# Gates of six tiles for both token halves at once in Strassen's form, and the branch projections kept in DRAM

## The chip, the core and the metric

The kernel runs on one core of one Trainium2 chip, as one program. The metric is device time in microseconds of one execution, as the median of several runs. PE is the matrix engine (TensorE), DVE the vector engine, ACT the scalar engine, POOL is GpSimd and SP is SyncE; the last two issue most of the DMAs.

## What is computed

One encoder layer on 1024 tokens of width 1024, in fp32. The reference, cut to what matters:

```python
mod = silu(c) @ w_ada + b_ada            # 6 vectors of 1024: sh1, sc1, gt1, sh2, sc2, gt2
h = rmsnorm(x, norm1_g) * (1 + sc1) + sh1
u, v, q, k, va, gate_a, gate_b = split(h @ w_in)
a_out = gmlp_branch(u, v, ...) @ w_a
b_out = window_attention_branch(q, k, va, ...) @ w_b
merged = sigmoid(gate_a) * a_out + sigmoid(gate_b) * b_out
x = x + gt1 * (merged @ w_o)
h2 = rmsnorm(x, norm2_g) * (1 + sc2) + sh2
f_gate, f_up = split(h2 @ w_ffn_in)
x = x + gt2 * ((silu(f_gate) * f_up) @ w_ffn_out)
```

The change is about `gate_a`, `gate_b` and `merged`. Both gates are 1024 x 1024 products of the same `h`.

## The kernel before

**Products.** Every fp32 operand is split into a rounded high part and a low part (`wh`/`wl` for weights, `h`, `mH`/`mL` and so on for activations), and a product is three matmuls: high by high, high by low, low by high (`mm3`, L154). Making a split costs a cast on ACT and a subtraction on DVE (a "low"): `unit` (L146) loads a 512 KB weight unit, casts it and subtracts. A 1024-deep product for one tile of 128 output channels (a d tile, eight of them) and 512 tokens is 8 x 3 = 24 matmuls of 128x512.

**Stages.** `half(hf)` (L511) runs the first sub-layer for one half of the tokens and is called twice. It has: the Q and K/V product over eight k tiles (L573 to L627); attention and the gMLP branch, with the `u` product and the gates of d tiles 0 and 1 put between as fillers (L716); then for each d tile the gate of branch b, the projection of branch b, the gate of branch a and the projection of branch a, 24 + 12 + 24 + 12 matmuls, where the sigmoid is a tanh on ACT, and the merge and its split are on DVE (L871 to L905; for d 0 and 1 only the projections); then the output projection, 24 matmuls a tile, with the residual, the sum of squares, the store of x1 to DRAM and the norm of what comes next (L922 to L958). In half 0 what comes next is half 1's `h`; in half 1 it is the first half of the FFN's input. After both halves comes the FFN: the gate and up products in Strassen's form (seven products of half blocks in place of eight, on both token halves at once, through sums of weights and of tokens), and the output product in the same form (L1437 on).

**The conditioning vectors.** `mod` is 48 columns. One column is a dot of a 128x1024 block of `w_ada` with `silu(c)` on DVE, a `tensor_tensor_reduce` (`ada_dot`, L204; the trace calls it CUSTOM_DVE_ANT_0). The sixteen columns of sc1 and sh1 are made in half 0's Q/K/V loop, two for each k tile; the other 32 by `ada_next` (L502), two or three for each d tile of the branch stage and two in the first output projection.

**What sets the order.** Where `in_order` is set, an engine keeps the order in which the code is written; elsewhere a scheduler places instructions. SP's loads always keep program order (`load`, L126). Stores go out on POOL (`store`, L129). Every instruction through the engine wrapper is recorded as line 75. The four `mm` banks and four `at` banks of PSUM, the four `tmp` buffers (tag `t2`) and the three buffers of each weight tag are reused in turn, and a new user waits until the last one is done.

Of the kernel before, what the change touches and what calls it, by code (L numbers as in the profile page):

```python
# [16 lines left out]
P = 128  # L17
# [17 lines left out]
FA, FB, FC = 2, 1, 4  # L35


@with_exitstack
def kernel(
# [153 lines left out]
    mod = const.tile([P, 48], F32, tag="mod", name="mod")  # L193
    SH1, SC1, GT1, SH2, SC2, GT2 = (8 * i for i in range(6))

    def ada_base():

        V.tensor_copy(base, bada)
        V.tensor_scalar(base[:, GT1:SH2], bada[:, GT1:SH2], 0.5, None, op0=ALU.mult)
# [4 lines left out]
    def ada_dot(r, col):  # L204

        factor = 0.5 if GT1 <= col < SH2 else 1.0
        for sc, g in ((SC1, g1c), (SC2, g2c)):
            if sc <= col < sc + 8:
                factor = g[:, col - sc : col - sc + 1]
        V.tensor_tensor_reduce(out=r, in0=r, in1=silu_c, op0=ALU.mult, op1=ALU.add, scale=factor,  # L210
                               scalar=base[:, col : col + 1], accum_out=mod[:, col : col + 1])

    def ada_pair(k):
        r = midt(F32, 2)
        load(r.rearrange("p a b -> p (a b)"), w_ada1[k])
        return r

    x1d = dram.tile([D, S], F32, tag="x1d", name="x1d")
    NP = NF // 2
# [280 lines left out]
    ada_queue = [b + i for b in (GT1, SC2, SH2, GT2) for i in range(8)]  # L500

    def ada_next(n):  # L502
        for _ in range(n):
            if ada_queue:
                col = ada_queue.pop(0)
                ada_dot(raw_unit(w_ada2[col - GT1]), col)
# [4 lines left out]
    def half(hf):  # L511
# [4 lines left out]
        if hf == 0:  # L516
            in_order[0] = True
            xt = [midt(F32, 1) for _ in range(3)]
            xt = [xt[k // 3][:, 0, k % 3 * 640 : (k % 3 + 1) * 640] for k in range(KT)]
            hl4 = midt(F32R, 16)  # L520
            base_bias = bias_base()
            build_bias(*base_bias, range(NH))
            A.activation(sm(QPK, "es"), ones[:, :QPK], AF.Silu)
            crow = load_cond()
            for k in range(KT):
                load(xt[k], xT[k * P : (k + 1) * P, :640])
# [6 lines left out]
            keep_going(total, identr, zeros, 22)  # L533
            ss = ss_tile()
            sqs = [midt(F32, 1)[:, 0, :] for _ in range(3)]
            for k in range(KT):
# [5 lines left out]
                if k == 1:  # L542
                    silu_cond(cond)
                    ada_base()
# [5 lines left out]
            ada_dot(r[:, 0, :], SC1)  # L550
            V.reciprocal(rcol[0], root)
            ada_dot(r[:, 1, :], SH1)
            wq = [wpool.tile([P, UNIT], F32R, tag=x, name=nm(x)) for x in ("wh", "wl")]
            A.copy(wq[0], wq0)
            wk = [wpool.tile([P, UNIT], F32R, tag=x, name=nm(x)) for x in ("wh", "wl")]
            A.copy(wk[0], wk0)
# [8 lines left out]
        else:  # L565
            hH, hL = h_next

        nkv = NT + 1 - 2 * hf
        qps = [mm_bank() for _ in range(NT)]
        if hf == 1:  # L570
            kbk = [at_bank() for _ in range(3)]
            kps = [kbk[t][:, :256] for t in range(nkv)]
        for k in range(KT):  # L573
            if hf == 0:
# [10 lines left out]
                if k == 0:  # L585
                    V.tensor_tensor(wq[1], wq0, wq[0].bitcast(F32), op=ALU.subtract)
                    V.tensor_tensor(wk[1], wk0, wk[0].bitcast(F32), op=ALU.subtract)
                A.activation(h4, x[:, HALF:], AF.Identity, bias=sh)
                A.activation(x[:, HALF:], x[:, HALF:], AF.Identity, bias=sh)
                if k == 0:  # L590
                    rb = ss_tile()
# [5 lines left out]
                if k < KT - 1:  # L597
                    ada_dot(r[:, 0, :], SC1 + k + 1)
                V.scalar_tensor_tensor(out=hL[k // 4][:, k % 4, :], in0=x[:, :HALF], scalar=sh,
                                       in1=hH[k // 4][:, k % 4, :].bitcast(F32),  # L600
                                       op0=ALU.add, op1=ALU.subtract)
                if k < KT - 1:
                    ada_dot(r[:, 1, :], SH1 + k + 1)
            elif k == 0:
                wq, wk = early.pop(0), early.pop(0)
            if k == 4:
                wk = unit(w_kv[1], V)
            if k % 2 == 1 and k < KT - 1:
                wq_next = unit(w_q[(k + 1) // 2], V)
# [8 lines left out]
            for group in ((q_parts, k_parts) if k == 4 else (q_parts + k_parts,)):  # L618

                for es in (((0,), (1,), (2,)) if hf + k == 0 else ((0, 1), (2,))):  # L620
                    for ps, st, w, o, n, first, last in group:
                        for e in es:
                            T.matmul(ps, st[e // 2], w[e % 2][:, o : o + n],
                                     start=k + e == 0 and first,
                                     stop=bool(k == KT - 1 and e == 2 and last))
# [3 lines left out]
        if hf == 0:  # L629
            attention_constants()  # L630
        else:
            col_rstd(sums[0], NT, rcol[2])
# [236 lines left out]
        mH = [None, None]  # L869
        mL = [None, None]  # L870
        for d in range(KT):  # L871
            if d % 4 == 0:
                mH[d // 4] = midt(F32R, 4)
                mL[d // 4] = midt(F32R, 4)
            ms = []
            in_order[0] = d < 2
            if d > 1:
                wg2 = unit(w_gb[d])
                wab = unit(w_ab[d])
                wg1 = unit(w_ga[d])  # L880
            else:
                wg1 = wg2 = None
                wab = units[9 + d]
            for (wg, o, br) in ((wg2, 512, (oH, oL)), (wg1, 0, (gH, gL))):
                sg = gate_act(gate(wg)) if d > 1 else sgs.pop(0)
# [648 lines left out]
```

## Time and profile before

| | |
|---|---|
| median of 3 runs | 1254.77 us (1254.21 to 1256.0) |
| profiled execution | 1255.57 us, of it the span 1253.8 us |
| granted TensorE clock | 1.000 |
| DMA | 214.25 MB, mean 171 GB/s |
| chain that ended last | PE 77%, issue 12%, DVE 5%, ACT 3%, DMA 2% |
| half 0: Q/K/V product | about 18.6 to 60.5 us |
| half 0: attention and gMLP | to about 168 us |
| half 0: branch projections with gates | to 276.8 us |
| half 0: output projection | to about 322 us |
| half 1: Q/K/V, attention, gMLP | to about 465 us |
| half 1: branch projections with gates | to about 576 us |
| half 1: output projection | to about 615 us |
| FFN gate and up products | to about 1050 us |
| FFN output product | to 1253.8 us |

Columns of a row of a timeline are start, duration, engine, line, operation, output and inputs by the program's names, shapes and count, and in square brackets how long the engine had been idle and who released it. Rows of groups have the sum and the mean duration of one in ns, and then the idle time in front of them. The busy time of a matmul overlaps with the next one's, so the time that one costs is read from a start to the next start.

### The profile page before, as it was taken

What the parts mean: (1) busy time and instruction counts of PE and PEld (TensorE: products, weight loads), DVE (VectorE), ACT (ScalarE), POOL (GpSimd) and SP (SyncE); (2) the same over time, 40 slices, a digit from 0 to 9 for tenths busy, and PEclk for the clock granted to TensorE, in tenths of its full rate; (3) what the DMA queues carried; (4) which work ended last, traced back from release to release, by engine and by line L of the source; (5) the groups of instructions that cost most, each with busy time, mean ns of one, the idle gap of its engine ahead of it and who ended that gap; (6) DMA issues with size and microseconds to landing.
All of it is one profiled execution on the core that took longest, in us unless ns stands there. A gap on an engine that the chain in (4) does not pass through costs nothing.

```text
span 1253.8 us, 15448 instructions
## 1 busy us (share of the span) xinstructions
PE 1240.1 (99%) x5749; PEld 1029.5 (82%) x5749; DVE 858.1 (68%) x1361; ACT 543.6 (43%) x867; POOL 133.6 (11%) x148
## 2 busy tenths in 40 slices
PE   8999999999999999999999999999999999999998
PEld 6888888888788888888888888888888888888887
DVE  9898875557458786656698756676666676455646
ACT  5467853324247772324444333333333334443442
POOL 1123310000032330000100000010110000010001
PEclk9999999999999999999999999999999999999999
DMA  9421145546522126557612354454654549886652
GB/s 368 164 89 64 51 147 181 183 158 219 178 77 68 52 84 200 185 178 242 240 48 94 141 201 143 160 201 185 218 173 178 187 168 337 296 325 192 193 168 101
DMA packets 67917, 214.25 MB, mean 171 GB/s; under 512 B 7809, under 2 KB 8065, under 8 KB 62594
## 3 DMA queue, kind: packets, MB, share of 16 engines
q1 hardware_dynamic: 56594, 155.59, 37.4%
q0 software_dynamic: 11248, 57.68, 12.4%
q8 instruction: 45, 0.74, 0.2%
q14 instruction: 30, 0.25, 0.1%
HBM read 170.24 MB, written 42.99 MB: 170 GB/s over the span
## 4 chain that ended last, share of the span: by engine, by line
PE 77%; issue 12%; DVE 5%; ACT 3%; DMA 2%; POOL 0%; DVEq 0%; ACTq 0%; POOLq 0%
PE mm L75 47%; PE at L75 30%; DVE mid L75 1%; DVE wl L75 1%; DMA wS<-wo 1%; ACT wh L75 1%; DMA wo<-in_w_out_dram 1%; ACT mid L75 1%; ACT lb L75 1%; DVE lb L75 0%; DVE ws L75 0%; DVE xs L75 0%; ACT pH L75 0%; ACT t L75 0%; ACT xs L75 0%
## 5 line engine op out<-in xcount | busy, mean ns | idle before, releaser
L75 ACT CAST wh<-raw 128x1024 fp32r<-128x1024 f32 x161 | 169.1, 1053 | 207.9 <-PE mm L75 100.1
L75 DVE TENSOR_TENSOR wl<-raw,wh 128x1024 fp32r<-128x1024 f32 x147 | 180.4, 1231 | 106.4 <-ACT wh L75 106.0
L75 PE MATMUL mm<-mid,wh 128*128 128x512 f32 x736 | 227.8, 390 | 0.8 <-DVE mid L75 0.6
L75 PE MATMUL mm<-h,wh 128*128 128x512 f32 x608 | 187.9, 390 | 0.0
L75 PEld LDWEIGHTS mm<-mid,wh 128*128 128x128 f32 x736 | 137.7, 188 | 30.4 <-DVE mid L75 1.0
L75 PE MATMUL mm<-mid,wl 128*128 128x512 f32 x368 | 143.3, 389 | 0.0
L75 PE MATMUL mm<-wh,h 128*128 128x512 f32 x384 | 128.7, 398 | 5.1 <-ACT h L75 2.8
L75 PEld LDWEIGHTS mm<-h,wh 128*128 128x128 f32 x608 | 113.7, 188 | 23.4
L75 PE MATMUL mm<-h,wl 128*128 128x512 f32 x304 | 118.3, 389 | 0.0
L75 DVE TENSOR_TENSOR wl<-ws,wh 128x1024 fp32r<-128x1024 f32 (+1 forms) x55 | 62.0, 1128 | 43.7 <-ACT wh L75 43.7
L75 PEld LDWEIGHTS mm<-wh,h 128*128 128x128 f32 x384 | 71.1, 188 | 20.6 <-ACT h L75 4.1
L75 PEld LDWEIGHTS mm<-mid,wl 128*128 128x128 f32 x368 | 69.1, 188 | 14.4
L75 ACT CAST wh<-ws 128x1024 fp32r<-128x1024 f32 (+1 forms) x55 | 53.6, 974 | 58.6 <-DVE ws L75 42.2
L75 PE MATMUL mm<-wl,h 128*128 128x512 f32 x192 | 74.6, 391 | 0.0
L75 PE MATMUL at<-h,wh 128*128 128x512 f32 x240 | 74.1, 390 | 0.0
L75 DVE CUSTOM_DVE_ANT_0 raw<-raw,silu_c,base 128x1024 f32<-128x1024 f32 x32 | 41.5, 1298 | 47.4 <-DMA raw<-in_w_ada_dram 45.5
L75 PEld LDWEIGHTS mm<-h,wl 128*128 128x128 f32 x304 | 57.1, 188 | 12.1
L75 DVE TENSOR_TENSOR ol<-raw,oh 128x1024 fp32r<-128x1024 f32 x30 | 36.6, 1224 | 35.7 <-ACT oh L75 31.7
L75 ACT ACTIVATE xs<-xs 128x512 f32<-128x512 f32 x21 | 13.3, 633 | 95.9 <-DVE xs L75 95.9
L75 PE MATMUL at<-wl,wh 128*128 128x512 f32 (+1 forms) x138 | 53.3, 386 | 0.0
L75 PE MATMUL at<-wh,wl 128*128 128x512 f32 (+1 forms) x138 | 53.3, 386 | 0.0
L75 PE MATMUL at<-wh 128*128 128x512 f32 (+1 forms) x138 | 53.3, 386 | 0.0
(243 smaller groups left out, 2464.3 us busy)
## 6 DMA issues: line engine op xcount, KB each, us to landing
raw<-in_w_ada_dram SPq DMA_DIRECT2D x32, 512.0 KB, 3.5
raw<-in_w_gate_dram SPq DMA_DIRECT2D x28, 512.0 KB, 4.1
tA<-hid POOLq DMA_DIRECT2D x11, 1024.0 KB, 4.9
tB<-hid POOLq DMA_DIRECT2D x11, 1024.0 KB, 5.3
wo<-in_w_out_dram POOLq DMA_DIRECT2D x22, 512.0 KB, 6.4
wS<-wo POOLq DMA_DIRECT2D x11, 1024.0 KB, 5.3
raw<-wS SPq DMA_DIRECT2D x44, 256.0 KB, 3.7
raw<-tB SPq DMA_DIRECT2D x44, 256.0 KB, 4.4
```

The lines of the kernel that those rows point to most:

```text
L75: ins = f(*args, **kw)
```

## The change

The gates of d tiles 2 to 7 leave `half`. Both halves now run only their attention and their branch projections one after the other. A branch result of d 0 or 1 is still merged at once (its gates come from the fillers) and stored in DRAM (`md`). A result of d 2 to 7 is copied by ACT out of PSUM and stored by POOL's queue (`pd`, 24 stores of 256 KB). Half 0's stage also normalises half 1's tokens, after the fifth d tile, since no output projection lies between the halves any more; the first-norm activations of both halves are stored too (`hd`, 4 MB), and half 1's stage loads them back and makes the sums of tokens that the seven products need.

Then `gate_products` runs, for d 2 to 7, seven products of 12 matmuls on half blocks, for both gates and both halves at once: 84 matmuls a tile. It makes sums of the weights of both gates, loads the four stored branch results of the tile, and merges. Both output projections follow; the first one no longer has a norm, the second one has it.

The conditioning dots become `scalar_tensor_tensor` with an accumulator. In the first loop each is finished by a 128x1 operation on ACT; the later ones are finished four at a time on DVE, from a copy of `silu(c)` in DRAM (`cd`, 512 KB) where it is needed after attention. They are spread differently: four in half 0's branch stage, twelve in half 1's Q/K/V loop, eight in the first output projection, eight in the FFN's output product.

In half 0's Q/K/V loop the warm-up of PE has 18 matmuls in place of 22, two of the eight rows of the attention bias are built after the loop, the first pair of `w_ada` blocks is loaded as two, the cast and the low of the first K/V weight come later, and the last K pass of k tile 0 and the K passes of k tile 4 run a step later.

The core of the diff:

```diff
+    def ada_dot(r, col, cast=None):
+
+        c1 = slice(col, col + 1)
+        V.scalar_tensor_tensor(
+            out=r, in0=r, scalar=1.0, in1=silu_c, op0=ALU.mult, op1=ALU.mult,
+            accum_out=acc_mod[:, c1],
+        )
+        if cast is not None:
+            A.copy(*cast)
+        factor, added = 1.0, bada
+        if GT1 <= col < SH2:
+            factor, added = 0.5, base
         for sc, g in ((SC1, g1c), (SC2, g2c)):
             if sc <= col < sc + 8:
-                factor = g[:, col - sc : col - sc + 1]
-        V.tensor_tensor_reduce(out=r, in0=r, in1=silu_c, op0=ALU.mult, op1=ALU.add, scale=factor,
-                               scalar=base[:, col : col + 1], accum_out=mod[:, col : col + 1])
+                factor, added = g[:, col - sc : col - sc + 1], base
+        A.activation(mod[:, c1], acc_mod[:, c1], AF.Identity, bias=added[:, c1], scale=factor)
...
+    def ada_late(r, col, row):
+
+        V.scalar_tensor_tensor(out=r, in0=r, scalar=1.0, in1=row, op0=ALU.mult, op1=ALU.mult,
+                               accum_out=acc_mod[:, col : col + 1])
...
+                if hf == 0 and (d, j) == (4, 1):
+                    col_rstd(ssn, NT, rcol[1])
+                if hf == 0 and (d, j) == (5, 0):
+                    rb = spread(rcol[1], NT)
+                if d < PLAIN_GATES:
+                    sg = sgs.pop(0)
+                    V.scalar_tensor_tensor(out=sg, in0=sg, scalar=1.0, in1=pb, op0=ALU.add, op1=ALU.mult)
+                    ms.append(sg)
+                else:
+                    p = tmp()
+                    A.copy(p, pb)
+                    store(pd[hf, d, 1 - j], p)
+            if d < PLAIN_GATES:
+                V.tensor_tensor(ms[0], ms[0], ms[1], op=ALU.add)
+                store(md[hf, d * P : (d + 1) * P, :], ms[0])
+            if hf == 1:
...
+            if d > 4:
+                for k in ((0, 1), (2, 3, 4), (5, 6, 7))[d - 5]:
+                    xk = xs[k // 4][:, k % 4, :]
+                    hi, lo = (t[k // 4][:, k % 4, :] for t in h_next)
+                    modulate(xk, rb, k, SC1, SH1, hi, lo, xk)
+                    store(hd[1, k * P : (k + 1) * P, :], xk)
...
+    def gate_sums(d, u):
+
+        if d < KT:
+            if not gsum:
+                gsum.append(fps[0].tile([P, UNIT], F32, tag="ru", name="gsum"))
+            w, g, r = gsum[0], ga_raw[d], gb_raw[d]
+            if u == 1:
+                V.tensor_tensor(w[:, Q:], r[:, :Q], r[:, Q:], op=ALU.add)
+                V.scalar_tensor_tensor(out=w[:, :Q], in0=w[:, Q:], scalar=-1.0, in1=g[:, :Q],
+                                       op0=ALU.mult, op1=ALU.subtract)
+            else:
+                V.tensor_tensor(w[:, Q:], g[:, :Q], r[:, :Q], op=ALU.add)
+                V.tensor_tensor(w[:, :Q], g[:, Q:], w[:, :Q], op=ALU.subtract)
+                load_gb(d + 1)
...
+        for d in GD:
+            banks = {}
+            for i, (u, part, t, b, first) in enumerate(STEPS):
+                if first:
+                    banks[b] = mm_bank() if b == "a" else at_bank()
+                multiply(gunits[d, u], part, gblk[t], banks[b], first)
+                bank = banks[b]
+                copies = i in (0, 2, 3)
+                if i == 0:
+                    s = tmp()
+                    A.copy(s, bank)
+                elif i == 2:
+                    v = tmp()
+                    A.copy(v, bank)
+                elif i == 3:
+                    c22 = tmp()
+                    A.copy(c22, bank)
+
+                if i == 0:
+                    gate_sums(d, 2)
+                    gate_high(d, 2)
+                elif i == 1:
+                    gate_low(d, 2)
+                elif i == 2:
+                    gate_high(d, 3)
+                    merge(s, ps[1, 0])
+                    gate_low(d, 3)
+                elif i == 3:
+                    gate_sums(d + 1, 1)
+                elif i == 4:
+                    gate_high(d + 1, 0)
+                elif i == 5:
+                    merge(c22, ps[0, 1])
+                elif i == 6:
+                    gate_high(d + 1, 1)
+                    merge(v, ps[0, 0])
+                    V.tensor_tensor(merged[0][d // 4][:, d % 4, :], v, c22, op=ALU.add)
+                    if d == KT - 1:
+                        split(merged[0][1][:, 3, :], mH[1][:, 3, :], mL[1][:, 3, :])
+                    gate_low(d + 1, 1)
+                run_tokens((0, 4, 4, 4, 0, 0, 0)[i])
...
+                if i == 1:
+                    V.tensor_tensor(s, bank, s, op=ALU.add)
+                    A.activation(s, s, AF.Tanh, scale=0.5)
+                elif i == 4:
+                    V.tensor_tensor(c22, bank, c22, op=ALU.add)
+                    A.activation(c22, c22, AF.Tanh, scale=-0.5)
+                    gate_low(d + 1, 0)
+                elif i == 5:
+                    V.tensor_tensor(v, bank, v, op=ALU.add)
+                    A.activation(v, v, AF.Tanh, scale=0.5)
+                elif i == 6:
+                    c21 = tmp()
+                    A.activation(c21, bank, AF.Tanh, scale=-0.5)
+                    merge(c21, ps[1, 1])
+                    V.tensor_tensor(merged[1][d // 4][:, d % 4, :], s, c21, op=ALU.add)
+                    ps = load_p(d + 1)
+        in_order[0] = False
+        return (mH, mL), merged[1]
...
+    m = gate_products(*half(1))
+    m = out_projection(0, *m)
+    out_projection(1, m, None)
```

DVE in the first Q/K/V loop, from the first normalised tile on (`mid_116` and `mid_121` are the x tiles, `h_241` the low part of h, `ss` the spread norm, ISA with `silu_c` a dot). Before:

```order
L75 SCALAR_TENSOR_TENSOR mid_116<-mid_116,mod,at_227 128x512
L75 SCALAR_TENSOR_TENSOR mid_116<-mid_116,mod,at_232 128x128
L75 TENSOR_TENSOR wl_217<-raw_149,wh_216 128x1024
L75 TENSOR_TENSOR wl_220<-raw_151,wh_219 128x1024
L75 ISA mid_247,mod<-mid_247,silu_c,base,cc 128x1024
L75 ISA mod 128x1
L75 SCALAR_TENSOR_TENSOR h_241<-mid_116,mod,h_239 128x512
L75 ISA mid_247,mod<-mid_247,silu_c,base 128x1024
L75 ISA mod 128x1
L75 SCALAR_TENSOR_TENSOR mid_116<-mid_116,mod,ss_256 128x640
```

And in the changed kernel, at the same place:

```order
L76 SCALAR_TENSOR_TENSOR mid_121<-mid_121,mod,at_227 128x512
L76 SCALAR_TENSOR_TENSOR mid_121<-mid_121,mod,at_232 128x128
L76 TENSOR_TENSOR wl_213<-raw_156,wh_212 128x1024
L76 SCALAR_TENSOR_TENSOR h_241<-mid_121,mod,h_239 128x512
L76 SCALAR_TENSOR_TENSOR mid_247,acc_mod<-mid_247,silu_c 128x1024 x2
L76 SCALAR_TENSOR_TENSOR mid_121<-mid_121,mod,ss_257 128x640
L76 TENSOR_TENSOR wl_215<-raw_158,wh_214 128x1024
L76 SCALAR_TENSOR_TENSOR mid_289,acc_mod<-mid_289,silu_c 128x1024
```

The two weight lows stood one behind the other ahead of the first h low; now the second stands behind the next tile, and a dot is one row without a second one for the sum.

DVE at the change of halves before (`t` is the evicted output projection with its residual, `ss` the sum of squares, `wl` the lows of half 1's first weights):

```order
L75 SCALAR_TENSOR_TENSOR t_552_2936<-mm_2908,mod,xs_2906 128x512
L75 TENSOR_TENSOR wl_2951<-raw_2948,wh_2950 128x1024
L75 TENSOR_TENSOR ss_2618<-ss_2618,t_553_2938 128x512
L75 SCALAR_TENSOR_TENSOR t_563_2986<-mm_2958,mod,xs_2956 128x512
L75 TENSOR_TENSOR wl_3023<-raw_3020,wh_3022 128x1024
L75 TENSOR_TENSOR ss_2618<-ss_2618,t_564_2988 128x512
```

ACT at the change of halves in the changed kernel (`t` is a copied branch result out of its bank, `h_2104` a part of half 1's h, `wh_2291` and those after it are weights of half 1's Q/K/V product):

```order
L76 COPY t_425_2193<-mm_2180 128x512
L76 ACTIVATE h_2104<-mid_1907,mod 128x512 x2
L76 COPY t_430_2227<-mm_2214 128x512
L76 ACTIVATE h_2104<-mid_1907,mod 128x512
L76 CAST wh_2291<-raw_2265 128x1024
L76 COPY t_432_2243<-mm_2230 128x512
L76 CAST wh_2349<-raw_2319 128x1024
L76 CAST wh_2382<-raw_2321 128x1024
```

The banks of the last projection tiles were freed by DVE, behind lows; now ACT frees them, and the last copy stands behind the cast of `wh_2291`, whose buffer the last projection still reads.

DVE in one d tile of the gates in the changed kernel, from the second bank's sum on (`t` gate banks and merges, `xs` and `hs` loaded branch results, `gsum` sums of weights, `mid` merged tiles); five rows more end the tile (a merge, the second merged tile, two sums, a 1024-wide low):

```order
L76 TENSOR_TENSOR t_879_4435<-at_4444,t_879_4435 128x512
L76 SCALAR_TENSOR_TENSOR t_879_4435<-t_879_4435,xs_4418 128x512
L76 TENSOR_TENSOR wl_4475<-raw_4300,wh_4474 128x512
L76 TENSOR_TENSOR gsum<-raw_4439 128x512
L76 SCALAR_TENSOR_TENSOR gsum<-gsum,raw_4340 128x512
L76 TENSOR_TENSOR t_889_4494<-mm_4422,t_889_4494 128x512
L76 TENSOR_TENSOR wl_4511<-raw_4340,wh_4510 128x1024
L76 SCALAR_TENSOR_TENSOR t_889_4494<-t_889_4494,hs_4416 128x512
L76 TENSOR_TENSOR t_884_4472<-at_4481,t_884_4472 128x512
L76 SCALAR_TENSOR_TENSOR t_884_4472<-t_884_4472,hs_4414 128x512
L76 TENSOR_TENSOR mid_4246<-t_884_4472,t_889_4494 128x512
L76 TENSOR_TENSOR wl_4544<-gsum,wh_4543 128x1024
```

One d tile of half 0's stage before, its gates, projections, dots and sum of squares for half 1:

```order
L75 TENSOR_TENSOR wl_2153<-raw_2150,wh_2152 128x1024
L75 SCALAR_TENSOR_TENSOR t_399_2077<-t_399_2077,mm_2079 128x512
L75 ISA raw_2253,mod<-raw_2253,silu_c,base 128x1024
L75 ISA mod 128x1
L75 TENSOR_TENSOR wl_2159<-raw_2156,wh_2158 128x1024
L75 TENSOR_TENSOR ss_1882<-ss_1882,t_407_2145 128x512
L75 ISA raw_2256,mod<-raw_2256,silu_c,base 128x1024
L75 ISA mod 128x1
L75 SCALAR_TENSOR_TENSOR t_402_2118<-t_402_2118,mm_2120 128x512
L75 TENSOR_TENSOR wl_2165<-raw_2162,wh_2164 128x1024
L75 TENSOR_TENSOR t_399_2077<-t_399_2077,t_402_2118 128x512
L75 TENSOR_TENSOR mid_1848<-t_399_2077,mid_1847 128x512
```

Lows of three 1024-wide weight units, two dots, two merges and the split of the merged tile stood beside 72 matmuls of one half; now three 1024-wide lows, a half-wide one and thirteen 512-wide sums and merges stand beside 84 matmuls of both halves.

More of the change, by code (lines that the diff above doesn't have):

```diff
@@ L1000 @@
+    half(0)
+    m = gate_products(*half(1))
+    m = out_projection(0, *m)
+    out_projection(1, m, None)
+    fp = fps[0]
+    B11, B21 = ((h2[0][0][q], h2[0][1][q]) for q in range(2))
+    T1, T2 = ((fpt(f"{n}h"), fpt(f"{n}l")) for n in ("tt1", "tt2"))
     RG, RU, U = {}, {}, {}
@@ L1050, in product @@
             banks[f, b] = mm_bank() if b == "a" and f % 6 > 1 else at_bank()
[L1051 to L1059 removed]
+        multiply(U[f, u], part, t, banks[f, b], first)
     def plain_row(f):
```

477 lines of the change are left out of this document (341 added, 136 removed).

## The prediction

> **What bounds the kernel now.** I read the page's busy shares first, then the windows by stage, then the chain of work that ended last, and only then single rows.
>
> ```profile
> span 1253.8 us, 15448 instructions
> PE 1240.1 (99%) x5749; PEld 1029.5 (82%) x5749; DVE 858.1 (68%) x1361; ACT 543.6 (43%) x867; POOL 133.6 (11%) x148
> ```
>
> PE is busy nearly everywhere, but that share is an average. The windows give, for each stretch, its length and then the busy time of PE, PEld, DVE, ACT and POOL, the granted clock, the DMA share and GB/s. In order these are: half 0's Q/K/V product, its branch projections with gates, its output projection, half 1's Q/K/V product, its branch stage, ten tiles of the FFN's first product, and the FFN's second product.
>
> ```profile
> 18.60:60.50 41.90, 38.09 (x216) 32.67 (x217) 38.18 (x54) 17.03 (x33) 5.67 (x8) 1.00 0.63 250
> 169.00:276.80 107.80, 107.80 (x477) 88.98 (x475) 62.63 (x82) 35.19 (x48) 0.00 (x0) 1.00 0.53 172
> 276.80:322.00 45.20, 45.20 (x208) 37.72 (x209) 30.91 (x43) 17.02 (x23) 4.84 (x7) 1.00 0.73 242
> 322.00:353.00 31.00, 29.39 (x162) 25.21 (x161) 9.59 (x10) 6.45 (x8) 1.08 (x2) 1.00 0.36 122
> 465.00:573.00 108.00, 108.00 (x477) 89.38 (x477) 66.01 (x90) 31.69 (x40) 0.00 (x0) 1.00 0.62 196
> 800.00:991.00 191.00, 190.84 (x842) 157.57 (x842) 128.47 (x179) 65.02 (x91) 16.68 (x31) 1.00 0.52 188
> 1050.00:1253.80 203.80, 199.81 (x888) 165.50 (x886) 112.60 (x113) 79.18 (x79) 8.80 (x15) 1.00 0.68 227
> ```
>
> The two stages that hold the gates have PE busy for all of their length, with DVE and ACT far below it. There a matmul taken out is time taken out. Only the first Q/K/V product is different: DVE is as busy as PE, and PE idles 41.90 − 38.09 = 3.8 us. The chain says the same of both gate stages and shows one hole, at the change of halves:
>
> ```profile
> 167.71 109.08 PE mm L75 x481
> ...
> 284.00 37.90 PE mm L75 x167
> ...
> 321.91 0.74 DVE t L75
> 322.65 0.81 DVE wl L75
> ...
> 325.10 0.72 PE mm L75 x2
> ```
> ```profile
> 464.81 111.62 PE mm L75 x491
> ```
>
> From here comes the price of one 128x512 matmul where PE never waits: 109.08 / 481 = 0.2268 us, and 111.62 / 491 = 0.2273 us.
>
> **Term 1, the products.** Six d tiles (2 to 7) times two gates times two halves times 24 matmuls are 576 before. Seven block products of 12 matmuls for each of the six tiles are 504 after. 72 matmuls × 0.2268 = **−16.3 us**, if the new stage keeps PE fed.
>
> Does it? The FFN already runs this very form: its window of ten tiles shows 12.8 us of DVE and 6.5 us of ACT per 19.1 us of PE, with no PE idle. For the gates I count one d from the order in the section on the change, with these rows:
>
> ```profile
> L75 DVE TENSOR_TENSOR wl<-raw,wh 128x1024 fp32r<-128x1024 f32 x147 | 180.4, 1231 | 106.4 <-ACT wh L75 106.0
> L75 DVE SCALAR_TENSOR_TENSOR t<-t,mm 128x512 f32<-128x512 f32 x32 | 21.9, 683 | 6.3 <-PE mm L75 6.3
> L75 ACT CAST wh<-raw 128x1024 fp32r<-128x1024 f32 x161 | 169.1, 1053 | 207.9 <-PE mm L75 100.1 <-PE at L75 35.4 <-issue 33.2
> L75 ACT COPY t<-mm 128x512 f32<-128x512 f32 x12 | 7.0, 587 | 15.7 <-PE mm L75 15.7
> ```
> ```profile
> L75 DVE SCALAR_TENSOR_TENSOR h<-hs,mod,h 128x512 fp32r<-128x512 f32 x8 | 5.8, 745 | 1.6 <-ACT h L75 1.6
> ```
>
> DVE has three 1024-wide lows and fourteen 512-wide operations: 3 × 1.231 + 14 × 0.683 = 13.3 us. ACT has three casts of 1.05, one half-width cast, three copies and four tanh of about 0.6: 8 us. PE needs 84 × 0.2268 = 19.05 us. PE stays the bound with 5.7 us to spare per tile; at the first and last d there are eight more lows or splits, 5.5 us of DVE, which just fits. I charge 0, at most 2.
>
> The stages without their gates get short: 24 matmuls or 5.44 us a tile. What must fit under them: in half 1 one low and five token operations, 1.23 + 5 × 0.68 = 4.6 us; in half 0, for d 5 to 7 together, 16 operations of 0.745 for half 1's norm and two lows, 14.4 of 16.3 us; in the first output projection, for d 2 to 5, a low, a split, an eviction, a sum and two dots, about 5.8 of 5.44 us, which the other four tiles give back. All are near the edge, so I charge 0 with an upper end of +3 us. A late eviction there reaches PE only after the four mm banks are full. The FFN's second product gets eight dots (10 us of DVE in 203.8 us where DVE is busy 112.6) and 4.5 MB of loads: 0, at most +1.
>
> **Term 2, the change of halves.** PE stood still before half 1's first K passes because bank copies on DVE were queued behind weight lows:
>
> ```profile
> 325.10 0.49 PE L75 MATMUL mm<-wh,h 128*128 128x512 f32 x1 [1.61 <-DVE t L75]
> ```
>
> Now the banks are freed by ACT copies of branch results. The fourth bank's copy stands behind one weight cast that itself waits for the last branch product: 1.05 + 0.59 = 1.64 us, against six 512-wide matmuls, 1.36 us, before PE needs it. So some 0.3 us stay and **−1.3 us** go (0 to −1.6: nothing, if the cast comes later still).
>
> **Term 3, the first Q/K/V product.** Here DVE's queue is the chain. A dot is one custom operation before:
>
> ```profile
> 20.25 1.48 DVE L75 CUSTOM_DVE_ANT_0 mid<-mid,silu_c,base 128x1024 f32<-128x1024 f32 x1
> 21.66 0.08 DVE L75 DVE_READ_ACCUMULATOR2_ANT mod<- 128x1 f32 x1
> 21.66 0.74 DVE L75 SCALAR_TENSOR_TENSOR h<-mid,mod,h 128x512 fp32r<-128x512 f32 x1
> 22.33 1.27 DVE L75 CUSTOM_DVE_ANT_0 mid<-mid,silu_c,base 128x1024 f32<-128x1024 f32 x1
> 23.53 0.08 DVE L75 DVE_READ_ACCUMULATOR2_ANT mod<- 128x1 f32 x1
> 23.53 0.88 DVE L75 SCALAR_TENSOR_TENSOR mid<-mid,mod,ss 128x640 f32<-128x640 f32 x1
> 24.33 1.33 DVE L75 CUSTOM_DVE_ANT_0 mid<-mid,silu_c,base 128x1024 f32<-128x1024 f32 x1
> ```
>
> Start to start the scale's dot takes 1.41 us and the shift's 1.20; the 512-wide scalar_tensor_tensor takes 0.67 and the 640-wide 0.80. So 128 columns cost 0.13 us, and 1024 wide is 0.67 + 4 × 0.13 = 1.19 us, an estimate: the trace of before holds no such dot. With an accumulator read of 0.08 it is up to 1.27. Fourteen dots in this stage (two lie ahead of it) save 14 × (1.31 − 1.19 to 1.27), so 0.5 to 1.7 us; I take 1.2. The late K passes may win back some of the 3.8 us of PE idle: I take 1.0.
>
> Against it stands the start. DMA is the limit there:
>
> ```profile
> 24.00:30.00 6.00, 5.02 (x29) 4.11 (x28) 6.00 (x9) 2.64 (x5) 0.69 (x1) 1.00 1.02 421
> 36.00:42.00 6.00, 5.93 (x34) 5.01 (x33) 6.00 (x8) 2.63 (x5) 0.78 (x2) 1.00 0.69 259
> ```
>
> At 421 GB/s the added store of silu(c), 0.5 MB, is 1.2 us of landings for all that follows it, and ACT casts the first weight ahead of the small operation that finishes the first scale. First h comes about 0.7 us later. **−1.5 us** in all (+2 to −4). The four dropped warm-up matmuls are worth nothing, as the matmuls behind them wait for the sum of squares, whose last addition is the one that ends at 13.8:
>
> ```profile
> 12.05 1.75 DVE L75 TENSOR_TENSOR ss<-ss,mid 128x640 f32<-128x640 f32 x2
> ```
> ```profile
> 14.04 1.17 PE L75 MATMUL at<-ones,ss 128*128 128x1 f32 x10
> ```
>
> **The sum.** The profiled execution took 1255.57 us (span 1253.8 and 1.8 us around it). −16.3 − 1.3 − 1.5 = −19.1 gives 1236.5. The median of the runs shown is 1254.77, 0.8 us lower, so I forecast **1235.7 us** for the median.
>
> **Rivals.**
>
> *Only the products count, and the short stages give some back:* 1255.57 − 16.3 − 0.8 = 1238.5, plus up to 5 us of late evictions: 1238.5 to 1244. For it: DVE is at 0.85 to 1.07 of PE's time in the short stages, and half 1's Q/K/V product goes from 9.59 us of DVE to 9.59 + 12 × 1.2 = 24 of 31 with its twelve dots. Against it: four banks of slack and the FFN's clean rows.
>
> *The start gains all it can:* PE's idle 3.8 us gone and term 2 whole, 1255.57 − 16.3 − 3.8 − 1.6 − 0.8 = 1233.1, down to 1231 if the first h isn't late.
>
> [...]
>
> *Slower: the stores of the branch results hold up the projections.* Each half's six late tiles put two results into four buffers, and a buffer is free only when its store on POOL's queue has landed.
>
> ```profile
> mid<-x1d POOLq DMA_DIRECT2D x4, 1024.0 KB, 12.7
> ...
> x1d<-t POOLq DMA_DIRECT2D x8, 256.0 KB, 4.7
> ```
> ```profile
> L130 POOL DMA_DIRECT2D x1d<-t x8 | 4.5, 566 | 41.9 <-DVE t L75 41.9
> ```
>
> Two buffers a tile, four in all: the tile's period is at least (0.59 copy + 0.57 issue + landing) / 2, and PE needs 5.44 us. It binds from a landing of 9.7 us. It eats the whole gain from 13 us, where twelve tiles lose (7.08 − 5.44) × 12 = 19.7 us; at 14.5 us they lose 28.7 and the time is 1235.7 + 28.7 = 1264. For it: the half 0 stage now moves some 13.5 MB (twelve weight and ada units of 0.5, x 2, branch results 3.5, h 2) in 43.5 us, 310 GB/s, where the saturated row above shows 421, and stores queue on POOL behind stores that wait for the norm. Against it: the nearest row lands in 4.7 us, less than half of what binds. [...]
>
> *The change doesn't do what it says:* the order shows 84 matmuls a tile and 72 fewer in all, so I leave this out.
>
> **Chances.** Forecast with its own spread (1233 to 1238.5) 0.60; products only 0.18; start gains all 0.11; half-rate dots 0.06; slow stores 0.05. The range 1231 to 1244 holds the first three, 0.89 as cases, less their misjudged sizes, say 0.8. A measurement here can tell about 0.2%, 2.5 us, from no change. Faster by more: the first three and a little of the half-rate case, 0.90. Within: the rest of the half-rate case, 0.05. Slower: the stores, 0.05.
>
> **What would show it.** Term 1: PE busy for the whole of the new gate stage, six tiles of 19.05 us, and no PE wait on a weight low or merge. Term 2: the first wait of half 1 under 0.5 us, on ACT. Term 3: dots of 1.2 to 1.3 us start to start, and the last Q/K/V matmul of half 0 about 1.5 us earlier than 60.5. The forecast is wrong if the new dots take 2.2 us, if the branch stages run longer than 16 × 12 matmuls, 43.5 us, or if PE shows waits on stores' buffers.

## The result and the profile after

| | median | range | runs | ratio to before |
|---|---|---|---|---|
| before, beside it | 1254.3 us | 1253.55 to 1256.0 | 5 | |
| changed kernel | 1243.94 us | 1241.14 to 1245.05 | 5 | 0.9913 [0.9902, 0.9925] |

The change takes 10.4 us, 0.87%. The forecast was 1235.7 us, 8.2 us lower than what came. The profiled execution took 1244.72 us, of it the span 1242.9.

The page's first part, of the changed kernel:

```profile
span 1242.9 us, 15585 instructions
PE 1227.1 (99%) x5673; PEld 1019.4 (82%) x5673; DVE 901.2 (73%) x1448; ACT 579.0 (47%) x945; POOL 158.1 (13%) x190
```

PE's busy time fell by 13.0 us, less than the products' 16.3; most of the difference is matmuls at a lower clock, shown below. The windows by stage, with the columns of before: half 0's Q/K/V product; half 0's branch projections; half 1's Q/K/V product; the gates of six tiles; the end of the gates (to 507.8 us), the first output projection and the second one's first tile; the second one's column sums and next tile.

```profile
18.60:60.80 42.20, 38.68 (x217) 33.70 (x218) 39.73 (x58) 23.71 (x51) 8.96 (x11) 0.96 0.84 322
167.80:212.00 44.20, 44.20 (x204) 36.81 (x204) 34.51 (x49) 24.15 (x37) 12.86 (x22) 1.00 0.83 291
212.00:244.00 32.00, 31.97 (x175) 27.47 (x174) 21.89 (x37) 7.22 (x9) 1.21 (x3) 1.00 0.76 304
396.00:504.60 108.60, 108.60 (x481) 89.80 (x479) 76.28 (x105) 49.35 (x75) 0.26 (x1) 1.00 0.37 117
504.60:557.00 52.40, 52.27 (x229) 42.66 (x228) 38.93 (x57) 19.49 (x28) 3.81 (x7) 1.00 0.76 263
557.00:572.30 15.30, 10.85 (x42) 9.15 (x42) 7.46 (x9) 6.09 (x8) 2.33 (x3) 0.78 0.59 199
```

Two rows have PE clearly below their length. The first is the old stage, with a clock of 0.96 that before did not show there. The other is new: in 15.3 us just behind the first output projection PE is busy for 10.85, and the clock is 0.78. PE's timeline names the wait:

```profile
561.53 1.83 PE L76 MATMUL at<-ones,ss 128*128 128x1 f32 x8 [4.45 <-DVE ss L76]
```

PE waits 4.45 us for the sum of squares, since the column sums of half 0's second norm stand between the second projection's first tile and its second. The chain of work that ended last, followed back from there (start, duration, what):

```profile
529.89 4.80 DMA raw<-in_w_o_dram
...
534.80 1.06 ACT wh L76
...
535.88 1.24 DVE wl L76
...
543.56 5.79 DMA raw<-in_w_o_dram
...
551.77 4.98 DMA raw<-in_w_gate_dram
...
560.87 0.61 DVE ss L76
...
561.53 1.83 PE at L76 x8
563.36 8.01 PE mm L76 x24
571.38 0.89 PE at L76 x8
```

It runs from load to load: a weight unit lands, is cast, its low is made, and only then has the next load its buffer. The last load in it is an FFN weight that PE does not need here. It reaches PE through the order of DVE's queue:

```profile
557.85 1.23 DVE L76 TENSOR_TENSOR first<-raw,first 128x1024 fp32r<-128x1024 f32 x1 [3.58 <-ACT first L76]
558.99 0.74 DVE L76 SCALAR_TENSOR_TENSOR t<-mm,mod,xs 128x512 f32<-128x512 f32 x1
```

The low of that weight stands ahead of the eviction of the first projection's last tile, which PE had finished at about 551.3 us, and the sum of squares needs that eviction. No run here moves that low.

Behind the wait the column sums take 1.83 us and the tile of 24 matmuls 8.01 us. In run 1 below, where PE does not wait there, they take 0.79 and 5.59:

```profile
557.05 0.79 PE at L76 x8
557.84 5.59 PE mm L76 x24
```

The hole therefore costs 4.45 + 1.04 + 2.42 = 7.9 us, and what stands behind the tile begins at 571.38 us in place of 563.43, 8.0 us later. That is the size of what is missing.

### The profile page after: what moved, and what is told of

Read it like the earlier page. It is cut to its first block, busy times and chain, and to the rows that moved or that the text cites. A ratio compares the mean times of both kernels' runs of the same rounds, so it can differ in the third digit from the quotient of the medians.

```text
span 1242.9 us, 15585 instructions
## 1 busy us (share of the span) xinstructions
PE 1227.1 (99%) x5673; PEld 1019.4 (82%) x5673; DVE 901.2 (73%) x1448; ACT 579.0 (47%) x945; POOL 158.1 (13%) x190
## 4 chain that ended last, share of the span: by engine, by line
PE 86%; DVE 6%; DMA 5%; ACT 2%; issue 1%; SPq 0%; DVEq 0%; ACTq 0%
PE mm L76 43%; PE at L76 42%; DVE mid L76 2%; DMA raw<-tA 2%; DVE wl L76 1%; DMA raw<-in_w_o_dram 1%; ACT wh L76 1%; DMA raw<-in_w_q_dram 1%; DVE h L76 1%; DVE t L76 0%; DVE ws L76 0%; DMA raw<-in_w_gate_dram 0%; DVE hid L76 0%; ACT lb L76 0%; DMA mid<-in_xT_dram 0%
## 5 line engine op out<-in xcount | busy, mean ns | idle before, releaser
L76 PE MATMUL mm<-mid,wh 128*128 128x512 f32 x704 | 219.5, 393 | 0.3
L76 DVE TENSOR_TENSOR wl<-raw,wh 128x1024 fp32r<-128x1024 f32 (+1 forms) x135 | 161.4, 1198 | 64.6 <-ACT wh L76 61.7
L76 ACT CAST wh<-raw 128x1024 fp32r<-128x1024 f32 (+1 forms) x149 | 153.9, 1034 | 113.2 <-PE mm L76 42.5
L76 PE MATMUL mm<-h,wh 128*128 128x512 f32 x400 | 124.0, 391 | 0.0
L76 PE MATMUL at<-h,wh 128*128 128x512 f32 x288 | 88.9, 390 | 0.0
L76 PEld LDWEIGHTS mm<-h,wh 128*128 128x128 f32 x400 | 74.7, 188 | 15.4
L76 PE MATMUL mm<-h,wl 128*128 128x512 f32 x200 | 77.9, 390 | 0.0
L76 ACT ACTIVATE t<-t 128x512 f32<-128x512 f32 x54 | 33.5, 631 | 85.7 <-DVE t L76 84.6
L76 PEld LDWEIGHTS at<-h,wh 128*128 128x128 f32 x288 | 54.0, 188 | 11.1
L76 ACT ACTIVATE xs<-xs 128x512 f32<-128x512 f32 x21 | 13.3, 632 | 95.4 <-DVE xs L76 95.4
L76 PE MATMUL at<-h,wl 128*128 128x512 f32 x144 | 56.1, 390 | 0.0
```

Source lines behind the costliest of these rows:

```text
L76: ins = f(*args, **kw)
```

## The experiments

Three questions stood open: is the hole made by the eight dots on DVE or by their loads; how much of it is the clock; and what did the start give.

**1 and 2: without the dots; loads without dots.** The first leaves out the eight sh2 columns of the first output projection, loads and dots; the second keeps their loads. In both, sh2 lacks its product with `w_ada`.

```diff
-                ada_next((0, 0, 2, 2, 2, 2, 0, 0)[d], cond)
+                if d == 2:
+                    V.tensor_copy(mod[:, SH2:SC2], bada[:, SH2:SC2])
```

The second has these two lines behind them, so that the rows are loaded and nothing reads them:

```diff
+                for _ in range((0, 0, 2, 2, 2, 2, 0, 0)[d]):
+                    raw_unit(w_ada2[ada_queue.pop(0) - GT1])
```

> The eight late conditioning dots (columns sh2) and their 512 KB loads leave the first output projection; sh2 then lacks its product with w_ada, so the output differs in that term. Theory (the three raw buffers, shared by weights of the projection and rows of w_ada, turn round too slowly, so the sum of squares that ends the first projection comes late): the 4.5 us wait of PE on ss and the slow matmuls behind it go, 8 us, 1243.9 to about 1236. Rival (the second output projection's start is bound by its own chain, whatever the dots do): under 2 us less.

> As e1, but the eight 512 KB loads stay and only the dots on DVE go (sh2 again lacks its product). Theory of the buffers: a loaded row that nobody reads gives its buffer back as it lands, so most of the 8 us go: 1236 to 1238. Rival one (DMA bandwidth in this stage): the bytes are the same, so 1242 to 1244. Rival two (DVE has too much work there): 1236.

Without both: 1236.42 us (1235.94 to 1236.89), ratio 0.9855 [0.9838, 0.9872]. With the loads alone: 1243.28 (1242.3 to 1243.97), 0.9909 [0.9891, 0.9927], the time of the changed kernel. Windows of 11 us, of the changed kernel, of the run without dots, and of the run with loads alone:

```profile
538.00:549.00 11.00, 11.00 (x50) 9.13 (x49) 6.96 (x11) 2.18 (x3) 0.83 (x2) 1.00 0.86 269
549.00:560.00 11.00, 8.08 (x35) 6.14 (x34) 7.10 (x11) 5.04 (x7) 0.79 (x2) 1.00 0.80 283
```
```profile
538.00:549.00 11.00, 11.00 (x51) 9.09 (x50) 5.21 (x7) 4.32 (x5) 1.08 (x2) 1.00 0.69 246
549.00:560.00 11.00, 11.00 (x54) 9.24 (x53) 6.89 (x8) 4.53 (x6) 2.16 (x3) 1.00 0.83 253
```
```profile
538.00:549.00 11.00, 11.00 (x50) 9.13 (x49) 3.24 (x5) 2.76 (x4) 1.08 (x2) 1.00 0.82 265
549.00:560.00 11.00, 7.94 (x36) 6.23 (x34) 6.68 (x8) 4.71 (x6) 1.08 (x2) 1.00 0.81 293
```

With the loads alone DVE works 3.24 of 11 us and PE still runs dry. So the hole is made by the loads, not by the dots' work on DVE, and a raw buffer that is freed late by a dot isn't needed for it either.

**3: the same eight, one for each of the eight tiles.**

```diff
-                ada_next((0, 0, 2, 2, 2, 2, 0, 0)[d], cond)
+                ada_next(1, cond)
```

> The same eight dots and loads, one for each of the eight tiles in place of two for tiles 2 to 5. Theory of the buffers: two loads a tile in three buffers, a turn of some 7.5 us for each, 5.0 us a tile, just under PE's 5.44: most of the wait goes, 1236 to 1239. Rival one (bandwidth) and rival two (DVE's work): bytes and work of the stage are unchanged, so 1242 to 1244.

1239.86 us (1237.79 to 1243.92), ratio 0.9877 [0.9854, 0.9899]. Some 4 us come back, with an uneven result: the profiled execution is the slowest, 1243.92, and PE still waits 3.5 us there. Spreading lowers what one tile asks for, not the bytes of the stage.

**4: PE kept busy through the hole.** 22 matmuls on an idle bank ahead of the column sums.

```diff
+                    idle = at_bank()
+                    for _ in range(22):
+                        T.matmul(idle, zeros, identr.unsqueeze(1).to_broadcast([P, 4, P]),
+                                 start=True, stop=True)
                     col_rstd(sums[0], NT, rcol[2])
...
```

> 22 idle matmuls of 128x512 on zeros stand ahead of the column sums that PE waits with, about 5.0 us of work in the 4.5 us hole. Theory (PE's clock was taken down behind the hole, and a dozen matmuls at 0.43 us cost 2.5 us on top of it): 1241 to 1242, granted clock in that stretch 1.00. Rival (the slow matmuls have another cause, such as operands): 1244 to 1245.

1243.22 us (1241.95 to 1243.82), ratio 0.9908 [0.989, 0.9926]. Its chain:

```profile
557.14 5.78 PE at L76 x30
562.92 5.59 PE mm L76 x24
```

The tile behind the hole takes 5.59 us in place of 8.01. The mechanism is there: the slow tile was the clock's, which was 0.50 from 562 to 568 us in the changed kernel, where a matmul took some 0.43 us from start to start, and 1.000 on average over this run, where the tile's take 0.233 (5.59 / 24). Over 560 to 571 us the clock was 0.69 behind the wait of 4.45 us in the changed kernel, 0.84 behind 3.8 us in run 2 and 0.69 behind 3.5 us in run 3; it was 0.84 behind waits of only 2.8 us in runs 5 and 8 and 1.6 us in run 6 too, and stayed at 1.00 behind 1.5 us in run 12. At the start it fell behind an idle time of 0.72 us in run 6 and stayed up behind 1.26 us in run 8 (last section), so the length of the wait alone does not decide. As for the time, the span is only 2.0 us shorter and the median 0.7 us, within both kernels' ranges, so the size of this part in the timed runs stays open.

**5: the rows in buffers of their own.** If the three raw buffers, which the weight units share with the `w_ada` rows, were the cause, rows in other buffers would cure it. The first row of a tile goes to a buffer beside the copy of silu(c), the second to two streamed half rows.

```diff
+                load(cond2[:, 1, :], src)
...
+                    t = stream("hs")
+                    load(t, src[:, cs])
...
+            acc2 = sm(8, "acc2")
-                ada_next((0, 0, 2, 2, 2, 2, 0, 0)[d], cond)
+                own_rows((0, 0, 2, 2, 2, 2, 0, 0)[d], cond2, acc2)
```

> All eight dots and loads stay in tiles 2 to 5 of the first output projection, with the same bytes; but the rows of w_ada load into buffers that stand free there (the other half of the tile with silu(c), and the two hs tiles, so every second dot is done in two halves), and the three raw buffers serve the projection's weights alone. Theory (with w, ada, ada turning through three buffers each weight load waits for the buffer of the weight ahead of it, so only one weight is in flight, 7 us a tile against PE's 5.44): the wait goes, 1236 to 1237.5. Rival (the DMA engines are too slow for this stage): 1242 to 1244.

1249.24 us (1248.12 to 1250.56), ratio 0.9965 [0.9953, 0.9978]: 5.3 us slower than the changed kernel, though PE's wait at the column sums is down to 2.8 us in its trace. Something else cost more; runs 11 and 12 found it.

**6, 7 and 8: the start, on top of run 5.** Run 6 sends the store of silu(c) at its place in the program, run 7 finishes the first scale ahead of the first weight's cast, run 8 does both.

```diff
-            store(cd, silu_c)
+            tc.keep_in_program_order(nc.gpsimd.dma_start(cd, silu_c))
...
-            ada_dot(r[:, 0, :], SC1, (wq[0], wq0))
+            ada_dot(r[:, 0, :], SC1)
...
+            A.copy(wq[0], wq0)
```

> e5, and the store of silu(c) to DRAM (512 KB) is issued behind the first Q/K/V loop in place of the start. Theory (that store pushed the first query weight's landing from 15.2 to 17.5 us, ACT's cast waits for it, and with it the first h): the weight lands at about 16.3, the loop ends 1.0 to 1.3 us earlier than 60.8, and the time is 1.0 to 1.3 us under e5. Rival (the loop's end is set by DVE's chain alone or by later loads): no change.

> e5, and ACT finishes the first scale and shift (two 128x1 operations) ahead of the cast of the first query weight, not behind it. Theory (DVE idles 1.4 us there for a number that is ready, and its chain sets the end of the loop): the first normalised tile starts at 17.5 in place of 18.9, the loop ends 1.0 to 1.4 us earlier, 1.0 to 1.4 us under e5. Rival (PE still waits for the cast weight): no change.

> e5 with the edits of e6 and e7 together. If both delays stand one behind the other, the sum: about 2 us under e5, 1234 to 1235. If the earlier weight makes the order of the cast unimportant: as the better of the two.

Run 5 took 1249.24 us; these took 1246.17 us (1244.13 to 1246.53), 1247.34 (1245.16 to 1248.81) and 1245.81 (1243.25 to 1247.41); ratios 0.9937 [0.9925, 0.9949], 0.9948 [0.9935, 0.996] and 0.9934 [0.992, 0.9947]. In run 6 the first weight is cast at 15.90 us, in run 5 at 17.22, so the store did delay it. Yet DVE then waits 1.5 us for PE, whose clock is down, and begins the first tile's tokens at 18.58 us, as late as the 18.59 of run 5:

```profile
15.00:17.00 2.00, 2.00 (x10) 1.71 (x10) 1.48 (x5) 1.37 (x3) 0.00 (x0) 0.61 1.03 414
17.00:19.00 2.00, 2.00 (x11) 1.96 (x11) 0.46 (x3) 0.42 (x2) 0.00 (x0) 0.54 1.07 436
```
```profile
15.00:17.00 2.00, 2.00 (x15) 1.68 (x15) 1.39 (x5) 0.59 (x3) 0.00 (x0) 1.00 1.02 414
17.00:19.00 2.00, 1.60 (x9) 1.04 (x8) 1.79 (x3) 2.00 (x4) 0.00 (x0) 1.00 1.06 432
```

The first two rows are run 6, the others run 8. Run 8's clock stayed at 1.00, and only there does the loop gain: its last long stretch of the Q/K/V product begins at 59.28 us, in run 5 at 60.58, in runs 6 and 7 at 60.56 and 60.74. What runs 6 and 7 gain on run 5 does not show in the loop; in their profiles PE's wait for the sum of squares is 1.6 and 1.5 us in place of 2.8, and why it shrank stays open. Both edits clear an obstacle at the start, but in these profiles the loop gained only where the clock stayed up.

**9 and 10: the rows moved to the gate stage; and the start.** Run 9 loads the eight rows and makes their dots in the stage of the gates, whose DMA share is 0.37. Run 10 adds run 8's two edits and a warm-up of 22.

```diff
+                    for j in {2: (0, 1, 2), 3: (0, 1, 2), 4: (1,), 5: (1,)}.get(d, ()):
+                        col = ada_queue.pop(0)
+                        load(rowbuf[j], w_ada2[col - GT1])
+                        waiting.append((rowbuf[j], col))
+                if i in (1, 3, 5) and waiting:
+                    ada_late(*waiting.pop(0), rowbuf[3])
...
-                ada_next((0, 0, 2, 2, 2, 2, 0, 0)[d], cond)
...
+            keep_going(total, identr, zeros, 22)
```

> The changed kernel with the eight dots and their loads moved out of the first output projection into the gate stage, tiles 3 to 6 (three, three, one, one), in parts of the merged tiles that are still empty there. Nothing else differs. Theory (the first output projection asks for more than its loads can bring: 2 MB a tile of 5.44 us; the gate stage asks for 2 MB in 19 us): as without the dots, 1236 to 1237, and no wait of PE on ss. Rival (DVE in the gate stage, 13.3 us of 19.05 plus up to 3.6, is then too slow): waits of PE in tiles 3 and 4, 1238 to 1241.

> e9, with the store of silu(c) behind the loop, scale and shift finished ahead of the first weight cast, and 22 warm-up matmuls as in the kernel before in place of 18. Theory (the edits of e6 and e7 gained nothing because PE's clock was at half in 15 to 19 us there, when it spreads the norm; e8, where it wasn't, ended the loop 1.4 us earlier; four more matmuls keep the clock): granted clock 1.00 in all of 11 to 27 us, the loop's last wait at 43.6 in place of 45.1, 1.2 to 1.6 us under e9, about 1235. Rival (the clock there is chance): half of the runs gain, 0.5 to 0.8 us under e9.

Run 9: 1236.81 us (1236.54 to 1237.08), ratio 0.9863 [0.9849, 0.9876], 7.1 us faster than the changed kernel, with all of its work in it. One tile of the gate stage in it, and then the place where the hole was:

```profile
434.00:453.00 19.00, 19.00 (x85) 15.73 (x84) 15.98 (x25) 7.50 (x11) 0.00 (x0) 1.00 0.56 198
...
557.00:572.30 15.30, 15.30 (x75) 12.88 (x75) 8.83 (x13) 5.37 (x8) 2.57 (x4) 1.00 0.59 204
```

The gate stage takes 4.5 MB more, the copy of silu(c) included, and DVE rises from 12.60 to 15.98 of 19.00 us, without a wait of PE; where the hole was PE is busy throughout, at a clock of 1.00.

Run 10: 1235.62 us (1234.78 to 1237.6), ratio 0.9856 [0.9842, 0.9869]. It is the fastest, 8.3 us below the changed kernel, but not apart from run 9. The longer warm-up did not hold the clock:

```profile
15.00:17.00 2.00, 2.00 (x12) 1.68 (x12) 1.47 (x4) 0.54 (x2) 0.00 (x0) 0.75 1.04 418
17.00:19.00 2.00, 2.00 (x11) 1.90 (x10) 0.78 (x3) 1.23 (x2) 0.00 (x0) 0.50 1.03 420
```

So the two start edits have no size of their own that these runs can tell.

**11: a small tile that nothing uses.** Run 5 and its three followers had one thing in common besides the rows, `acc2`, eight columns in the pool of small tiles, which shifts the pools behind it. Run 11 adds such a tile, and nothing else, to the changed kernel.

```diff
+    pad = small.tile([P, 8], F32, tag="pad", name="pad")
+    V.memset(pad, 0.0)
```

> The changed kernel with an unused tile of 8 columns in the pool of small tiles, which moves the pools laid out behind it by 128 bytes a partition, as the extra sum tile of e5 to e8 did. Theory (in e5 to e8 only matmuls whose moving operand lies in the FFN's pool cost 233 ns in place of 227, so it is that operand's address): about 700 matmuls by 6 ns, 4 us more than the changed kernel, 1247 to 1249. Rival (the slower matmuls came from the two-part dots or the chip): 1243 to 1245.

1250.24 us (1249.03 to 1251.58), ratio 0.9971 [0.9959, 0.9983], 6.3 us slower than the changed kernel. The chain in the FFN's first product, in the changed kernel and in run 11:

```profile
827.68 2.72 PE at L76 x12
...
833.12 2.72 PE at L76 x12
...
838.56 38.08 PE at L76 x168
```
```profile
827.36 2.79 PE mm L76 x12
830.15 2.80 PE at L76 x12
...
841.21 38.59 PE at L76 x168
```

Some products of twelve matmuls take 2.79 us in place of 2.72, with PE alone in the chain from 800 to 1000 us and a mean granted clock of 0.996 over the run, as in the changed kernel. They are those whose moving operand (the first input in a matmul's row, here a token block or a sum of token blocks) lies in the FFN's pool. Run 12, without such a tile, has 2.72 at the same place, and run 9, on the same chip as run 11, took 1236.81 us as a whole. The tile is run 11's only edit; that it slows these matmuls through the addresses of the pools behind it is the author's reading, since no trace shows an address.

**12: run 5 without the shift.** The second sums go into columns of `base` that are no longer used.

```diff
-            acc2 = sm(8, "acc2")
+            acc2 = base[:, SH2:SC2]
```

> e5 with the eight extra sums in columns of an existing tile that nothing else uses, so that no pool moves. Theory as it now stands (e2 and e5: the first output projection waits for its DMA transfers, whoever reads them and wherever they land; buffers are the smaller part): the wait of PE on ss stays at 2 to 4 us and the time is 1240 to 1244. Rival (the three shared raw buffers were the cause, and e5 only looked bad because of the moved pools): 1236 to 1238. Both say that the matmuls of the FFN cost 227 ns again.

1239.35 us (1239.03 to 1241.5), ratio 0.9885 [0.9867, 0.9902]. PE's wait behind the first output projection was 4.45 us in the changed kernel; here it is (sum, times, longest):

```profile
PE at L76 <- DVE ss L76: 1.5, 1, 1.5
```

Buffers of their own bring back 4.6 us and leave 2.5 us to run 9, between what either expectation said. So both seem to be at work: too much to load, and the shared buffers through which a late row makes the next weight late. How much each would cost alone stays open, since the halves also changed the size of the transfers.

## Why the prediction was right and where it was wrong

*What bounds the kernel, and term 1.* Right. The gates' window shows PE busy for 108.60 of 108.60 us, and DVE at 76.28 of them, which is 13.4 us in a tile's 19.05 where 13.3 were counted. The 72 matmuls are gone and their 16.3 us with them. Half 0's branch stage took 45.3 us, from 167.8 to 213.05, where the prediction had named 43.5 as a limit; the 16 small matmuls of half 1's norm, 1.7 us, stand in it now, and PE does not wait. Runs 1 and 9, where PE does not wait behind the first output projection, end at 1236.4 and 1236.8, within 1.1 us of the forecast. That they come so near is in part luck: term 3 fell short by 1.6 us, and 1.1 us of gains that were not forecast (0.3 in term 2, and 0.8 named below) made up for most of it.

*Term 2, the change of halves.* Right, and 0.3 us better: no idle time of PE shows ahead of half 1's first K passes. ACT did what the term said, a cast that waited for the last branch product and the bank's copy behind it:

```profile
213.02 1.06 ACT L76 CAST wh<-raw 128x1024 fp32r<-128x1024 f32 x1 [0.39 <-PE mm L76]
213.98 0.57 ACT L76 COPY t<-mm 128x512 f32<-128x512 f32 x1
```

*Term 3, the start.* Mis-sized: −1.5 us forecast, +0.1 measured. The last long stretch of PE in the Q/K/V product, before and after:

```profile
60.68 10.89 PE mm L75 x48
```
```profile
60.82 10.91 PE mm L76 x48
```

The dots themselves did as the term said, as their group shows:

```profile
L76 DVE SCALAR_TENSOR_TENSOR mid<-mid,silu_c 128x1024 f32<-128x1024 f32 x28 | 34.0, 1236 | 0.9 <-DMA mid<-in_w_ada_dram 0.9
```

What failed is "first h comes about 0.7 us later". The first weight was cast 2.1 us later, the scale only behind it, and DVE idled:

```profile
17.48 1.05 ACT L76 CAST wh<-raw 128x1024 fp32r<-128x1024 f32 x1 [1.89 <-DMA raw<-in_w_q_dram]
18.43 0.38 ACT L76 ACTIVATE mod<-acc_mod,base,cc 128x1 f32<-128x1 f32 x1
```
```profile
18.85 1.01 DVE L76 SCALAR_TENSOR_TENSOR mid<-mid,mod,at 128x512 f32<-128x512 f32 x2 [1.42 <-ACT mod L76]
```

In before that row of DVE began at 17.05 us: 1.8 us late, not 0.7. This is 1.1 of the 1.6 us; the rest stays open, with a clock down to 0.50 between 23 and 25 us as a candidate. In run 8 that row begins at 17.20 us, and the last stretch at 59.28, 1.4 us earlier than before. The warm-up "worth nothing" was not shown to be worth anything either: the clock in this stretch fell in run 10 with 22 as well as with 18, to 0.50 in both.

*The short stages.* This step failed. For the first output projection it priced DVE only, "about 5.8 of 5.44 us, which the other four tiles give back", and charged 0 with an upper end of 3 us. The loads had no price. It also said that a late eviction reaches PE only after the four `mm` banks are full; the last one reached PE sooner, through the sum of squares. These are the rows of the loads and the store in the DMA view of the whole execution (size, median time to landing):

```profile
raw<-in_w_ada_dram SPq DMA_DIRECT2D x20, 512.0 KB, 6.3
...
raw<-in_w_o_dram SPq DMA_DIRECT2D x16, 512.0 KB, 4.9
...
xs<-in_xT_dram SPq DMA_DIRECT2D x16, 256.0 KB, 4.4
...
x1d<-t POOLq DMA_DIRECT2D x8, 256.0 KB, 5.1
```

A tile of d 2 to 5 asks for two rows, one weight unit, a piece of x and a store: 2.1 MB in 5.44 us, 385 GB/s. The two 11 us windows of the changed kernel above show 269 and 283 GB/s at a DMA share of 0.86 and 0.80. PE ran dry only behind the stage, so the lag was paid at once, 4.45 us, and the clock made 8.0 us of it. The window of before for the same stage, quoted in the prediction, held the warning: 242 GB/s at a share of 0.73 are 331 GB/s for a full share, an estimate, below 385.

*Rivals.* "Only the products count" reached to 1244 and is closest by its number. Its late evictions did come, but they waited for loads, not for DVE's work, as run 2 shows. That 1243.94 still lies inside the range, by 0.06 us, is luck: two of the five executions, 1244.72 and 1245.05, lie above it. The "half-rate dots" of the chances fall with the group above: no run shows the 2.2 us each that would have spoken for them, the 28 dots take 1.236, and from the rows without a sum the prediction had estimated 1.19. The slow stores fall too: half 0's branch stage has PE busy for 44.20 of 44.20 us, and the stores landed, in the median, well below the 9.7 us that would bind:

```profile
pd<-t POOLq DMA_DIRECT2D x24, 256.0 KB, 4.6
```

*The account* of the profiled executions, 1255.57 to 1244.72 = −10.85 us: −16.3 products, −1.6 change of halves, +0.1 start, +8.0 hole, and −0.8 for a wait of PE that before had (a matmul begun at 463.82 us, the next at 464.81, where 0.23 us is usual) and that is gone: −10.6. About 0.3 us is not assigned.

## What to carry to other kernels

When work is moved into a shortened stage, divide the bytes that the stage loads and stores by its new length as well as counting its engines' work, and hold that against the rate that windows of a like mix show, not against the best window: here 385 GB/s were asked for where 269 and 283 came. The gate stage, with a DMA share of 0.37, took such loads for nothing: in run 9 PE is busy for 19.00 of 19.00 us in each of the tiles that got them. Look also at what stands ahead of an eviction in its engine's queue: here a low that DVE stood idle for, 3.58 us, held up the eviction behind it. And a wait of PE can be paid a second time in the clock, here behind waits from 1.6 to 4.45 us, though not behind 1.5 us in run 12. When an edit that adds a tile makes the kernel slower, compare the time of one matmul far from the edit, here 0.2325 us against 0.227, before looking for a wait.

## What the hardware showed that was not expected

*Addresses.* A tile of 128 bytes a partition (eight columns in each of its pool's four buffers) that nothing uses cost 6.3 us. In run 11 matmuls whose moving operand lies in the FFN's pool take some 233 ns from start to start (2.79 / 12 = 0.2325 us), in the changed kernel 227; the others kept 227. Run 12, with the same work as run 5 and no shift, is 9.9 us faster than run 5; some 3 us of that is the hole, which was 2.8 us with a slow tile of 7.18 us behind it in run 5 and 1.5 with 5.59 in run 12. That the address decides is an inference from these runs; which property of it was not tried.

*The clock at the start.* In run 6 the clock was at 0.61 and 0.54 from 15 to 19 us although PE's longest idle time behind the warm-up was 0.72 us:

```profile
14.13 1.28 PE L76 MATMUL at<-ones,ss 128*128 128x1 f32 x10 [0.72 <-DVE ss L76]
```

In run 8, with an idle time of 1.26 us at the same place, it stayed at 1.00 from 15 to 27 us; in the changed kernel it fell between 21 and 27, to 0.50. What sets the moment stays open.

*The rate of mixed transfers.* In the first output projection the DMA engines moved 269 GB/s at a share of 0.86, in the start 420 at 1.03: 313 and 408 GB/s for a full share, both estimates. Why the same busy time carries fewer bytes there was not settled.
